# Nearest 2x upsampling on one core: half of the input as two equal loads from two queues

## The chip, the core and the metric

The kernel runs on one core of one Trainium2 chip. The metric is the device time of one launch in microseconds (us); lower is better. The core has 16 DMA engines, which all transfers share. DMAs are issued here from three engines' queues: SyncE's (SP), ScalarE's (ACT) and GpSimd's (POOL). The copies are made by VectorE (DVE) and ScalarE. TensorE does no work.

## The reference

The input x is float32 of shape (16, 64, 64, 64), the scale factor is 2. Every pixel is repeated in a 2 by 2 block:

```python
result = np.zeros((batch, channels, 2 * h, 2 * w), dtype=np.float32)
for i in range(2 * h):
    for j in range(2 * w):
        result[:, :, i, j] = x[:, :, i // 2, j // 2]
```

So 16.78 MB are read and 67.11 MB written, and nothing is calculated.

## The kernel before

All image rows of x (16 x 64 x 64 of them, 64 pixels or 256 bytes each) are spread over the 128 partitions: partition p has R = 512 rows, which lie next to each other in HBM, 128 KB in all. In the output the same partition has 512 KB next to each other. One tile `mem` in each partition holds a free stretch of WF elements and, behind it, all of the partition's input, `xt`.

**Loads** (line 195). Four loads, all issued by SyncE, bring x in by ranges of rows in each partition, cut at 0, 8, 256, 480 and 512. In each partition that makes pieces of 2 KB, 62 KB, 56 KB and 8 KB. They are called loads 0 to 3 below. They wait for nothing. After the program is built, `begin_before_barrier` (line 13) takes the first EARLY = 4 instructions of SyncE, which are these loads, and puts them ahead of the barrier at the program's start.

**Copies** (lines 215 and 216). The 512 rows are worked through in nine groups of 52, 40, 52, 63, 52, 64, 63, 63 and 63 rows. In each group VectorE expands the first 9/16 of the rows and ScalarE the rest; each makes from a row of 64 pixels two rows of 128, so that a group of k rows fills k x 1 KB in each partition. The first group covers rows 0 to 52, the second rows 52 to 92, the third rows 92 to 144.

**Where the copies go.** Groups with an even number (0, 2, 4, 6, 8) go to the start of `mem`. Groups with an odd number go to a place that ends at the group's own first input row, over input that earlier groups have used up. A group at the start of `mem` must wait until the store of the group before it in that place has read its data, and the same holds for the other place, so two stores can be on their way at a time.

**Stores** (lines 218 and 222). Each group's store follows its copies. Groups 0, 1, 7 and 8 are stored from SyncE's queue, groups 2 to 6 from GpSimd's. The store of group 0 has one more dependency, added by hand: it waits for `loads[-2]`, which is the load of rows 256 to 480, so that stores begin as the loads end. SyncE issues in order, so store 1 stands behind store 0.

`close_early` (line 80) rewrites the program's end; the change doesn't touch it.

Of the kernel before, what the change touches and what calls it, by code (L numbers as in the profile page):

```python
# [6 lines left out]

EARLY = 4  # L10


def begin_before_barrier(nc):

    blocks = nc.main_func.blocks
    main, body = blocks[0], blocks[1]
    sp = mybir.EngineType.SP
    loads = [i for i in body.instructions if i.engine == sp][:EARLY]  # L20
    for load in loads:
        assert isinstance(load, mybir.InstDMACopy), type(load)
        assert not (load.sync_info and load.sync_info.on_wait)
    names = [i.name for i in loads]
    body.instructions = [i for i in body.instructions if i.name not in names]
    kept = list(main.instructions)
    at = next(
        n
        for n, i in enumerate(kept)
        if i.engine == sp and isinstance(i, mybir.InstDrain)  # L30
    )
    kept[at:at] = loads
    main.instructions = kept


def close_on_gpsimd(nc):
# [117 lines left out]
@with_exitstack  # L154
def kernel(
    ctx: ExitStack,
    tc: tile.TileContext,
    x: bass.AP,
    scale_factor: int,
    out: bass.AP,  # L160
):
    nc = tc.nc
    nc.at_finalize(begin_before_barrier)
    nc.at_finalize(close_early)
    P = nc.NUM_PARTITIONS
    s = int(scale_factor)
    B, C, H, W = x.shape
    R = B * C * H // P
    fdt = x.dtype

    xp = x.rearrange("b c h w -> (b c h) w").rearrange("(p r) w -> p r w", p=P)
    op = out.rearrange("b c (h hd) w -> (b c h) (hd w)", hd=s).rearrange(
        "(p r) w -> p r w", p=P
    )

    rows = [52, 40, 52, 63, 52, 64, 63, 63, 63]
    GROW = s * s
    FREE = 79
    WF = FREE * GROW * W
    assert sum(rows) == R
    mem_pool = ctx.enter_context(tc.tile_pool(name="mem", bufs=1))
    mem = mem_pool.tile([P, WF + R * W], fdt, name="mem")
    xt = mem[:, WF:].rearrange("p (r w) -> p r w", r=R)

    HEAD = 8
    cuts = [0, HEAD, R // 2, R - 32, R]
    loads = [
        nc.sync.dma_start(out=xt[:, lo:hi], in_=xp[:, lo:hi])  # L195
        for lo, hi in zip(cuts, cuts[1:])
    ]

    def expanded(r0, r1):
        return (  # L200
            xt[:, r0:r1].unsqueeze(2).unsqueeze(4).to_broadcast([P, r1 - r0, s, W, s])
        )

    r0 = 0
    before = (0, 0)
    for n, k in enumerate(rows):
        size = k * GROW * W
        at = 0 if n % 2 == 0 else WF + r0 * W - size
        assert at >= before[1] or at + size <= before[0]
        before = (at, at + size)  # L210
        u = mem[:, at : at + size].rearrange(
            "p (k a w b) -> p k a w b", k=k, a=s, w=W
        )
        kv = k * 9 // 16
        nc.vector.tensor_copy(out=u[:, :kv], in_=expanded(r0, r0 + kv))  # L215
        nc.scalar.copy(out=u[:, kv:], in_=expanded(r0 + kv, r0 + k))  # L216
        if 2 <= n < len(rows) - 2:
            store = nc.gpsimd.dma_start(  # L218
                out=op[:, r0 : r0 + k, :], in_=u, single_packet=True
            )  # L220
        else:
            store = nc.sync.dma_start(out=op[:, r0 : r0 + k, :], in_=u)  # L222
        if n == 0:
            tc.add_manual_dep(
                store.ins,
                loads[-2].ins.name,
                mybir.DependencyInfo(
                    mybir.DependencyClass.Sync, mybir.DependencyReason.DATA
                ),
                reason="stores begin as the loads end",  # L230
            )
        r0 += k
# [35 lines left out]
```

## Time and profile before

| | before |
|---|---|
| median of 3 runs | 197.26 us (197.16 to 197.34) |
| span of the profiled execution, first to last instruction | 195.8 us |
| between the span and the median of the runs | 1.5 us |
| DMA: packets, bytes, mean rate over the span | 1872, 83.89 MB, 428 GB/s |
| VectorE busy | 69.6 us (36%), 9 copies |
| ScalarE busy | 51.4 us (26%), 9 copies and a table load |
| GpSimd busy | 3.0 us (2%) |

The profile is one execution. Of it only the span is listed; the execution's own time on the device is not shown beside it, so the 1.5 us between the span and the median of the runs stand for what lies around the span. The busy time of the DMA engines is given by queue as a share of all 16 engines' span: q1 is the queue that SyncE issues to, q0 GpSimd's. A packet is one partition's row of one transfer, and 4 bytes for each engine of a transfer that report its end.

### The profile page before, as it was taken

What the parts mean: (1) busy time and instruction counts of PE and PEld (TensorE: products, weight loads), DVE (VectorE), ACT (ScalarE), POOL (GpSimd) and SP (SyncE); (2) the same over time, 40 slices, a digit from 0 to 9 for tenths busy, and PEclk for the clock granted to TensorE, in tenths of its full rate; (3) what the DMA queues carried; (4) which work ended last, traced back from release to release, by engine and by line L of the source; (5) the groups of instructions that cost most, each with busy time, mean ns of one, the idle gap of its engine ahead of it and who ended that gap; (6) DMA issues with size and microseconds to landing.
All of it is one profiled execution on the core that took longest, in us unless ns stands there. A gap on an engine that the chain in (4) does not pass through costs nothing.

```text
span 195.8 us, 108 instructions
## 1 busy us (share of the span) xinstructions
DVE 69.6 (36%) x9; ACT 51.4 (26%) x10; POOL 3.0 (2%) x9
## 2 busy tenths in 40 slices
DVE  0000596000039289069007205930692002960000
ACT  2000548000036083063920006666000003900000
POOL 0000000000000100100100100010000000000000
DMA  9999889699899989899999899999999999999994
GB/s 391 493 415 415 375 387 551 295 455 522 348 442 418 537 370 500 370 422 422 422 422 522 348 522 428 428 428 428 422 422 422 422 422 422 448 514 501 435 422 211
DMA packets 1872, 83.89 MB, mean 428 GB/s; under 512 B 208, under 2 KB 208, under 8 KB 336
## 3 DMA queue, kind: packets, MB, share of 16 engines
q1 hardware_dynamic: 1152, 45.35, 53.8%
q0 software_dynamic: 720, 38.54, 45.4%
HBM read 16.78 MB, written 67.11 MB: 428 GB/s over the span
## 4 chain that ended last, share of the span: by engine, by line
DMA 73%; DVE 15%; issue 1%; SPq 1%; DVEq 0%; POOLq 0%
DMA out_dram<-mem 54%; DMA mem<-in_x_dram 19%; DVE mem L215 15%; SPq L195 0%; SPq L222 0%; DVEq L215 0%; POOLq L218 0%; POOLq L263 0%
## 5 line engine op out<-in xcount | busy, mean ns | idle before, releaser
L215 DVE COPY mem<-mem 128x8960 f32<-128x8960 f32 (+3 forms) x9 | 69.6, 7739 | 104.9 <-DMA out_dram<-mem 83.1
L216 ACT COPY mem<-mem 128x7168 f32<-128x7168 f32 (+2 forms) x9 | 50.1, 5572 | 117.5 <-DMA out_dram<-mem 89.8
L218 POOL DMA_DIRECT2D out_dram<-mem x5 | 2.8, 560 | 126.8 <-DVE mem L215 111.2
L216 ACT ACT_TABLE_LOAD x1 | 1.3, 1283 | 2.2 <-PEq L249 2.2
L249 POOL MEMSET const-float32-0.0<- 128x1 f32 x1 | 0.1, 99 | 0.2 <-issue 0.2
L249 POOL MEMSET const-bfloat16-1.0<- 128x1 bf16 x1 | 0.1, 102 | 0.0
L249 POOL MEMSET const-float32-1.0<- 128x1 f32 x1 | 0.1, 99 | 0.0
L249 POOL MEMSET const-uint8-127<- 128x1 uint8 x1 | 0.1, 99 | 0.0
## 6 DMA issues: line engine op xcount, KB each, us to landing
out_dram<-mem POOLq DMA_DIRECT2D x2, 8064.0 KB, 29.9
out_dram<-mem SPq DMA_DIRECT2D x2, 8064.0 KB, 24.8
out_dram<-mem POOLq DMA_DIRECT2D x2, 6656.0 KB, 22.6
mem<-in_x_dram SPq DMA_DIRECT2D x1, 7936.0 KB, 21.3
mem<-in_x_dram SPq DMA_DIRECT2D x1, 7168.0 KB, 37.8
out_dram<-mem SPq DMA_DIRECT2D x1, 6656.0 KB, 18.1
out_dram<-mem SPq DMA_DIRECT2D x1, 5120.0 KB, 29.7
mem<-in_x_dram SPq DMA_DIRECT2D x1, 1024.0 KB, 39.8
```

The source lines that it names most:

```text
L215: nc.vector.tensor_copy(out=u[:, :kv], in_=expanded(r0, r0 + kv))
L216: nc.scalar.copy(out=u[:, kv:], in_=expanded(r0 + kv, r0 + k))
L218: store = nc.gpsimd.dma_start(out=op[:, r0 : r0 + k, :], in_=u, single_packet=True)
L249: nc = _bacc.Bacc("TRN2", target_bir_lowering=False, num_devices=1)
```

## The change

The four loads are cut at 0, 128, 256, 480 and 512 rows, so that the first half of x comes as two loads with pieces of 32 KB in each partition. The second of these, rows 128 to 256, is issued by ScalarE; the others stay with SyncE. The function that moves loads ahead of the barrier now does so for two engines: three loads of SyncE and one of ScalarE. The last two loads, and with them the dependency of store 0, are as before. Copies and stores are untouched.

```diff
-EARLY = 4
+EARLY = {mybir.EngineType.SP: 3, mybir.EngineType.Activation: 1}
...
-    loads = [i for i in body.instructions if i.engine == sp][:EARLY]
...
+    for engine, count in EARLY.items():
+        loads = [
+            i
+            for i in body.instructions
+            if i.engine == engine and isinstance(i, mybir.InstDMACopy)
+        ][:count]
+        assert len(loads) == count
+        assert not any(i.sync_info and i.sync_info.on_wait for i in loads)
+        names = [i.name for i in loads]
+        body.instructions = [i for i in body.instructions if i.name not in names]
+        kept = list(main.instructions)
+        at = next(
+            n
+            for n, i in enumerate(kept)
+            if i.engine == engine and isinstance(i, mybir.InstDrain)
+        )
+        kept[at:at] = loads
+        main.instructions = kept
...
-    HEAD = 8
-    cuts = [0, HEAD, R // 2, R - 32, R]
+    cuts = [0, R // 4, R // 2, R - 32, R]
+    queues = [nc.sync, nc.scalar, nc.sync, nc.sync]
     loads = [
-        nc.sync.dma_start(out=xt[:, lo:hi], in_=xp[:, lo:hi])
-        for lo, hi in zip(cuts, cuts[1:])
+        queue.dma_start(out=xt[:, lo:hi], in_=xp[:, lo:hi])
+        for queue, lo, hi in zip(queues, cuts, cuts[1:])
     ]
```

More of the change, by code (lines that the diff above doesn't have):

```diff
@@ L18, in begin_before_barrier @@
     main, body = blocks[0], blocks[1]
-    sp = mybir.EngineType.SP
-    loads = [i for i in body.instructions if i.engine == sp][:EARLY]
[L21 to L33, printed above, removed]
+    for engine, count in EARLY.items():
[16 more added lines that the diff above has]
+        main.instructions = kept
 def close_on_gpsimd(nc):
```

## The prediction

> **What bounds the kernel now.** I read the page's busy slices and queue shares first, then the DMA issues, then the chain of waits in order of time, then the timeline of the first 40 us, and last the trace's records of single DMA packets (one record is one partition's row on one of the 16 DMA engines).
>
> ```profile
> DMA  9999889699899989899999899999999999999994
> DMA packets 1872, 83.89 MB, mean 428 GB/s; under 512 B 208, under 2 KB 208, under 8 KB 336
> q1 hardware_dynamic: 1152, 45.35, 53.8%
> q0 software_dynamic: 720, 38.54, 45.4%
> HBM read 16.78 MB, written 67.11 MB: 428 GB/s over the span
> ```
>
> 53.8% and 45.4% make 99.2%: the DMA engines are busy for all but 1.6 us of the 195.8 us span, while VectorE is busy 36% and ScalarE 26%. The digits under 9 among the slices come from whole rows being booked at one moment; in the packet records each engine starts its next row 2 to 20 ns after the last, from the first load to the last store. The kernel is bound by the bytes, and the loads are the first fifth of them.
>
> ```profile
> mem<-in_x_dram SPq DMA_DIRECT2D x1, 7936.0 KB, 21.3
> mem<-in_x_dram SPq DMA_DIRECT2D x1, 7168.0 KB, 37.8
> mem<-in_x_dram SPq DMA_DIRECT2D x1, 1024.0 KB, 39.8
> mem<-in_x_dram SPq DMA_DIRECT2D x1, 256.0 KB, 2.6
> ```
>
> The last column is the time from issue to landing. With SyncE's four issues at 0, 0.42, 0.89 and 1.36 us the loads land at 2.64, 21.74, 38.68 and 41.16 us. Load 2 (7168 KB, 7.34 MB) takes 16.94 us behind load 1: 433 GB/s. That is the full rate, and by it all 83.89 MB need 193.6 us.
>
> ```profile
> 0.89 37.79 DMA mem<-in_x_dram
> 38.68 0.02 issue
> ...
> 39.29 29.69 DMA out_dram<-mem
> ...
> 79.15 40.20 DMA out_dram<-mem x2
> ...
> 129.52 35.38 DMA out_dram<-mem
> ```
>
> The chain runs from load 2 into store 0 and from there through later stores and three copies. Each copy in it (9.5 us on VectorE) has another transfer beside it, which is why the DMA engines never pause although the chain names VectorE for 15%.
>
> ```profile
> 0.00 1.80 SPq L195 DMA_DIRECT2D mem<-in_x_dram  x4
> ...
> 2.20 1.28 ACT L216 ACT_TABLE_LOAD   x1 [2.20 <-PEq L249]
> 21.77 5.10 ACT L216 COPY mem<-mem 128x5888 f32<-128x5888 f32 x1 [18.29 <-DMA mem<-in_x_dram]
> 21.84 10.89 DVE L215 COPY mem<-mem 128x7424 f32<-128x7424 f32 x2 [21.84 <-DMA mem<-in_x_dram]
> 29.81 4.03 ACT L216 COPY mem<-mem 128x4608 f32<-128x4608 f32 x1 [2.95 <-DVE mem L215]
> 38.77 136.12 SPq L222 DMA_DIRECT2D out_dram<-mem  x4
> ```
>
> Both engines start their first copies as load 1 lands and are through the first two row groups at 33.84 us (29.81 + 4.03). Store 0 then waits 4.9 us more for load 2, by the dependency set in the code.
>
> **How much there is to win.** The first packet starts at 1.0 us, and the last store's data ends 0.4 us before the span does. Between them lie 195.8 - 1.0 - 0.4 = 194.4 us against 193.6 us at the full rate, so 0.8 us are lost on the whole. They are lost at the very start. Load 0 (0.262 MB) needs 0.61 us at the full rate; its packets begin at 1.005 us and the slowest engine's end at 2.289 us, 0.68 us too long: six engines show a first row of 2 KB that took 368 to 587 ns where the later ones took 84. Load 1 needs 18.75 us and lands 19.10 us after load 0: 0.35 us too long, and its records show where: the first row of 62 KB takes 2382 to 3082 ns, 2680 on the mean, against 2342 for nearly all that follow. The slowest engine loses 1.0 us by this, the mean engine 0.8 us. From load 2 on nothing is lost: its rows take 2116 ns from the first, 27.1 bytes per ns.
>
> **The change part by part.**
>
> Bytes and number of loads stay: 32 + 32 + 56 + 8 KB of each partition's row in place of 2 + 62 + 56 + 8, four loads both times. At the full rate the sum for the loads is the same 38.7 us. Zero, and nothing has to hide it.
>
> Issue. SyncE loses one of four issues (0.43 us) and ScalarE gains one. SyncE's last load is issued at about 0.89 us instead of 1.36 us; it is served only after 37.8 us, so these 0.47 us are worth nothing. ScalarE's issue lies ahead of the barrier that releases it at 2.12 us in the trace of before; it reaches that barrier 0.13 us into the span, so an issue of about 0.4 us fits. Its table load follows the barrier and ends by 3.5 us, and its first copy comes 18 us later. If that cover were gone, it would cost the issue's 0.4 us. Its load is ready at about 1.2 to 1.6 us, while SyncE's first row of 32 KB keeps each engine until at least 1.0 + 1.2 = 2.2 us (32,768 bytes at 27.1 per ns). So no engine waits for ScalarE's issue.
>
> [...]
>
> Landing order. In the stretch from 152.5 to 162 us of before, where a store of GpSimd's queue and one of SyncE's run together, each engine serves one row of the one queue and one of the other, in turn, at 2380 to 2404 ns a row against 2380 alone. By that row loads 0 and 1 share the engines evenly and land together, after 64 KB per partition: 8.39 MB at 433 GB/s is 19.4 us, plus 1.0 us for the first packet, up to 1.0 us of the start and 0.35 us of completion, 21.0 to 21.8 us. The first two row groups (rows 0 to 92) now need load 0 alone; they are ready at about 33.1 to 33.9 us, still 5 us ahead of load 2. Row group 2 (rows 92 to 144) needs both and waits for store 0's space until 56.9 us anyway. Load 2 has the same bytes ahead of it, whatever the order, and store 0 the same load ahead of it; load 3's 1.05 MB (2.4 us) still covers store 0's issue, which came 38.77 us in while the engines were busy with load 3 to 40.3 us.
>
> The start. This is the one term that can move. The trace of before has no cold first row of 32 KB and no two loads side by side. From below: if a cold start with large rows pays only what load 1's first row paid, 0.35 us, the 0.68 us of the small load go away: -0.68 us. From above: if the whole 1.0 us is the price of sixteen engines starting on HBM at once, whatever the row, and ScalarE's queue pays a first row of its own at the mean excess of load 1's (2680 - 2342 = 0.34 us), the change costs +0.34 us. I take the row that is nearest, the cold start as one whole, paid once: 1.0 us before and 1.0 us after, less 8 rows at 84 against 76 ns, -0.07 us. I round that to nothing, since the unevenness between engines alone is 0.5 us there.
>
> Row switches between the queues: 16 rows per engine, each between 0 and 24 ns more by the mixed stores, 0 to 0.4 us. Most of those rows were at 2380, so I take 0.05 us.
>
> Sum: 0 + 0 - 0.07 + 0.05, about no change on a span of 195.8 us. The runs shown have a median of 197.26 us, 1.5 us above the span, which I leave as it is: 197.3 us. About 0.2% (0.4 us) is what a measurement of this kernel can tell from no change.
>
> **The rivals.**
>
> Faster: the 2 KB rows are the cost. For it: six of sixteen first small rows are 4 to 7 times too long, and a big row has time to hide such a delay. Against: the big rows behind them were again up to 0.74 us late, as if the start were shared and not the small rows' own. Price -0.68 us, 196.6 us.
>
> Slower: ScalarE's queue starts cold in the middle of SyncE's stream, and reads from HBM switch queues less freely than the stores did. Place: the first 20 us. Price: the first row of the second queue costs 0.34 us (mean) to 0.74 us (3082 - 2342, worst engine), and 16 switches up to 24 ns add up to 0.4 us: 0.4 to 1.1 us, 197.7 to 198.4 us. It decides from a loss of 0.025 us per row on each engine (16 rows, 0.4 us). [...] A fixed price for a second hardware queue outside the span would end on the same side. Against: mixed stores show almost nothing.
>
> Slower by far: SyncE's queue is served ahead of ScalarE's. Then load 1 would come only after loads 0, 2, 3 and stores 0 and 1 (24.6 MB, 57 us), and row group 2 would be copied with idle engines: 9.7 us of load 1, then 7.9 us of copy uncovered, about +8 us, 205 us. Against: the even turns of the two stores.
>
> The change not doing what it says: ScalarE's load after the barrier, at 2.2 us rather than 0.1. Eight rows of load 0 keep every engine until at least 10 us, so nothing changes; this is within the forecast.
>
> **How the numbers follow.** No change to be told 0.42; the small rows' price gone, faster, 0.22; the second queue's price, slower, 0.34; starvation, slower, 0.02. The range takes the faster end at 196.6 us and the slower rival up to 198.2 us; what is beyond each end I hold at 1 in 10.
>
> **What would show it.** Right: DMA slices at 9 throughout, loads 0 and 1 landing within about 1.5 us of each other near 21 us, load 2 at 38.4 to 39.0 us, store 0 issued right after, first copies near 21.5 us, and the end shifted by as much as load 2's landing. Wrong on the start: load 2's landing moved by more than 0.4 us, with first rows of 32 KB far from 1.2 us. Wrong on the switches: rows in the first 20 us longer than 1.21 us all along. Wrong outside: an equal span and another time. Wrong on the order: load 0 landing at 11 us, with load 1 either at 21 us (harmless) or after the first stores.

## Result: 0.28% slower, by what the stores lost

The changed kernel has a median of 197.95 us over 22 executions (197.77 to 198.31), the kernel before 197.23 us over 22 on the same chip. The ratio is 1.0028, with a 95% interval of 1.0019 to 1.0038: slower, by more than the 0.2% that count as no change. The executions of before come in two groups, which the numbers below need: 15 of the 22 lie between 197.03 and 197.34 us (short, below) and the others from 197.59 us upwards (long), while the changed kernel has none under 197.77 us. The profile of before fits the first group: its span is 195.8 us, and the changed kernel's profiled execution took 197.91 us on the device with a span of 196.58 us, 1.33 us around it, which puts the profiled execution of before at 197.1 us.

These lines of the page of the changed kernel answer to those of before:

```profile
DMA  8999999799899989899999899999999999999994
DMA packets 1873, 83.89 MB, mean 427 GB/s; under 512 B 209, under 2 KB 209, under 8 KB 209
q1 hardware_dynamic: 1008, 41.16, 48.8%
q0 software_dynamic: 720, 38.54, 45.5%
q10 hardware_dynamic: 144, 4.19, 4.9%
```

A third queue, q10, carries ScalarE's 4.19 MB. The three shares still sum to 99.2%: the DMA engines are as busy as before, for a span that is 0.8 us longer. So they are not idle for that time; they take longer for the same bytes.

Its DMA issues (KB each, us from issue to landing) and the start of its timeline:

```profile
mem<-in_x_dram SPq DMA_DIRECT2D x1, 7168.0 KB, 38.4
mem<-in_x_dram SPq DMA_DIRECT2D x1, 4096.0 KB, 21.9
mem<-in_x_dram ACTq DMA_DIRECT2D x1, 4096.0 KB, 21.9
mem<-in_x_dram SPq DMA_DIRECT2D x1, 1024.0 KB, 40.4
```

```profile
0.00 1.32 SPq L196 DMA_DIRECT2D mem<-in_x_dram  x3
0.12 0.38 ACTq L196 DMA_DIRECT2D mem<-in_x_dram  x1
...
21.89 10.89 DVE L216 COPY mem<-mem 128x7424 f32<-128x7424 f32 x2 [21.89 <-DMA mem<-in_x_dram]
29.87 4.03 ACT L217 COPY mem<-mem 128x4608 f32<-128x4608 f32 x1 [2.88 <-DVE mem L216]
38.89 136.73 SPq L223 DMA_DIRECT2D out_dram<-mem  x4
```

The change does what it says: ScalarE issues 0.12 us in, and both halves land together, at 21.87 and 22.04 us. VectorE's first copy begins 0.05 us later than before, and the copies of the first two row groups are through 5 us ahead of store 0's issue. Load 2 lands at 38.80 us (before: 38.68), load 3 at 41.28 us (before: 41.16).

The chain of waits, in order of time, shows where the rest comes from:

```profile
0.43 38.37 DMA mem<-in_x_dram
...
39.36 29.87 DMA out_dram<-mem
...
79.41 40.53 DMA out_dram<-mem x2
...
130.10 35.55 DMA out_dram<-mem
```

Leg by leg against before: load 2 lands 0.12 us later; store 0 takes 29.87 us for 29.69 (+0.18), the next two stores 40.53 for 40.20 (+0.33), the next 35.55 for 35.38 (+0.17). Together 0.80 us, the whole difference of the spans. The copies between the legs are the same. Five sixths of the loss fall into stores, which the change didn't touch.

The packet records say how (a record is one partition's row; the records don't name the engine, so I joined each to the one that ended just before it; where two engines end within a few ns of each other this can take one for the other, so counts and sums over all engines are surer than what is said of a single one). Store 0's rows of 52 KB: 1966 ns for every one of 128 in the kernel before, 1974 ns on the mean in the changed one. Store 1's rows of 40 KB: 1514 against 1522 ns. It begins with store 0's first row on each engine: in before, each engine goes from load 3 into store 0 within 6 ns; in the changed kernel 13 of the 16 first rows are 34 to 48 ns too long, and the engines had run out of load 3 for 0.11 us on the mean before their store rows came. Of store 0's later rows 78% are 2 to 12 ns too long (before: none), and it goes on so to the end. Each engine has 72 store rows. Beyond the row times of 1966, 1514, 2380 and 2418 ns (the usual times of rows of 52, 40, 63 and 64 KB), these add up to 0.61 us on the mean engine after the change and to 0.09 us before. Of the 0.61 us, 0.25 us lie in rows that are 1 to 12 ns too long, 0.15 us in rows 13 to 30 ns too long, and 0.21 us in 58 rows, the 13 first ones among them, that are 31 to 105 ns too long.

On the mean engine, then: 0.01 us from the loads, 0.11 us of idling ahead of store 0 and 0.52 us in store rows; and the slowest engine, which sets the end, lies 0.34 us behind the mean one, where it was 0.16 us.

### The profile page after: what moved, and what is told of

Same layout as the page of the kernel before. It is cut to its first block, busy times and chain, and to the rows that moved or that the text cites. A ratio compares the mean times of both kernels' runs of the same rounds, so it can differ in the third digit from the quotient of the medians.

```text
span 196.6 us, 108 instructions
## 1 busy us (share of the span) xinstructions
DVE 69.6 (35%) x9; ACT 51.4 (26%) x10; POOL 3.0 (2%) x9
## 3 DMA queue, kind: packets, MB, share of 16 engines
q1 hardware_dynamic: 1008, 41.16, 48.8%
q10 hardware_dynamic: 144, 4.19, 4.9%
## 4 chain that ended last, share of the span: by engine, by line
DMA 73%; DVE 14%; issue 1%; SPq 0%; DVEq 0%; POOLq 0%
DMA out_dram<-mem 54%; DMA mem<-in_x_dram 20%; DVE mem L216 14%; SPq L223 0%; SPq L196 0%; DVEq L216 0%; POOLq L219 0%; POOLq L264 0%
```

## Experiments

Three theories were on the table. A: ScalarE's queue, once used, costs at every later row. B: without the small first load the engines stand to each other so that their store rows collide. C, formed on the first four runs: store 0's rows reach some engines after these have run out of load 3, and such an engine pays at every row afterwards. The comparisons of each set ran on one chip, with the kernel before beside them.

**First set: which part of the change?**

Of the kernel before beside this set 14 of 29 executions lie at 196.99 to 197.22 us and 15 at 197.51 to 199.48. By the medians, then, three of the four runs can't be told from it: the ratios are 1.0001 for the halves from SyncE, 1.0008 for the small load from ScalarE and 1.0000 for the half from GpSimd, each with an interval of 0.0022 to either side. What they say rests on their profiles, and on how many of their executions are long.

Halves from SyncE alone:

```diff
-EARLY = {mybir.EngineType.SP: 3, mybir.EngineType.Activation: 1}
+EARLY = {mybir.EngineType.SP: 4}
-    queues = [nc.sync, nc.scalar, nc.sync, nc.sync]
+    queues = [nc.sync, nc.sync, nc.sync, nc.sync]
```

> The loads are cut into 32 + 32 + 56 + 8 KB rows as in the changed kernel, but all four are issued by SyncE; ScalarE's queue is not used. Theory A (once ScalarE's queue has been used, every later row on a DMA engine costs 5 to 8 ns more, 72 store rows each engine): store rows are back at 1966 ns (52 KB) and 1514 ns (40 KB), time within 0.1 us of before, 197.2 us. Theory B (the small first load sets the engines apart in a way in which their store rows don't collide, whatever the queue): store rows stay at about 1974 and 1522 ns on the mean and the time at 197.8 to 198.0 us.

Measured: 197.73 us median; 3 of 12 executions at 197.05 to 197.17 us, the others at 197.67 to 197.85. In the profile (an execution of 197.73 us) store 0's rows take 1969 ns and 5 engines have a long first row. Neither A nor B as stated: without ScalarE's queue store rows are too long on some engines and 9 of 12 executions are long, and the other quarter takes the time of before's short ones with the 32 KB rows in place.

The cuts of before, with load 1 on ScalarE's queue:

```diff
-    cuts = [0, R // 4, R // 2, R - 32, R]
+    cuts = [0, 8, R // 2, R - 32, R]
```

> The loads are cut into 2 + 62 + 56 + 8 KB rows as before; load 1 (62 KB rows) alone moves to ScalarE's queue. Theory A (ScalarE's queue): store rows at about 1974 and 1522 ns, time 197.8 to 198.0 us. Theory B (the small first load): rows of 1966 and 1514 ns, 197.2 us. Here SyncE's loads 2 and 3 also run beside load 1, so load 2 lands earlier relative to the end of the loads; by both theories this moves the time by less than 0.2 us, since the DMA engines stay busy.

Measured: 205.08 us. My remark that loads 1 and 2 side by side would move the time by less than 0.2 us was wrong, as its page and timeline show:

```profile
GB/s 386 425 380 467 492 380 380 386 0 335 502 335 425 515 425 335 502 525 418 405 405 370 502 335 540 412 412 412 409 405 507 507 405 405 405 405 405 456 557 203
```

```profile
38.95 5.10 ACT L217 COPY mem<-mem 128x5888 f32<-128x5888 f32 x1 [35.93 <-DMA mem<-in_x_dram]
38.95 10.89 DVE L216 COPY mem<-mem 128x7424 f32<-128x7424 f32 x2 [38.95 <-DMA mem<-in_x_dram]
46.91 135.74 SPq L223 DMA_DIRECT2D out_dram<-mem  x4
```

Load 1 shares the engines with load 2 and lands at 38.9 us together with it. The first copy begins only then, store 0 is issued at 46.91 us in place of 38.77, and the DMA engines stand still in the ninth slice. In this kernel the first copies need everything up to row 52, and load 1 has that. The run tells nothing about A and B; it shows that a load moved to the second queue no longer lands ahead of the load that stood behind it.

The small load alone on ScalarE's queue:

```diff
-    cuts = [0, R // 4, R // 2, R - 32, R]
-    queues = [nc.sync, nc.scalar, nc.sync, nc.sync]
+    cuts = [0, 8, R // 2, R - 32, R]
+    queues = [nc.scalar, nc.sync, nc.sync, nc.sync]
```

> As before in cuts; the small load of 2 KB rows alone moves to ScalarE's queue, which then has 0.26 MB to bring and nothing after 3 us. Theory A in its plain form (the queue's having been used is enough): store rows at about 1974 and 1522 ns, 197.7 to 198.0 us. Theory B (the engines' places after the start decide): the small rows are still there, but beside the 62 KB rows and not ahead of them, so a time between 197.2 and 197.9 us, with the store rows slow or not according to how the engines stand to each other.

Measured: 197.87 us, all 12 executions at 197.77 to 198.00. Load 2 lands at 38.81 us, 10 engines have a long first row in store 0, and its rows take 1973 ns. That is what A in its plain form expected, and B allowed it; this run doesn't decide between them.

Rows 128 to 256 from GpSimd's queue:

```diff
-EARLY = {mybir.EngineType.SP: 3, mybir.EngineType.Activation: 1}
+EARLY = {mybir.EngineType.SP: 3}
-    queues = [nc.sync, nc.scalar, nc.sync, nc.sync]
+    queues = [nc.sync, nc.gpsimd, nc.sync, nc.sync]
```

> As the changed kernel, but rows 128 to 256 are loaded from GpSimd's queue, behind the barrier, and not from ScalarE's. The stores use GpSimd's queue anyway, so no third queue is ever used. Theory A (ScalarE's queue): store rows at 1966 and 1514 ns, 197.2 us. Theory B (no small first load): slow store rows, 197.8 to 198.0 us. If any second queue in the load phase spoils the stores: slow rows too, and then it is the first run that tells which.

Measured: 197.73 us, one execution of 12 at 197.05, the others at 197.57 to 197.86. Three engines have a long first row in store 0; store 0's rows take 1968 ns on the mean, more than A expected and less than B. Joined by engine, 3 engines have 0.56 to 0.72 us too much in their 72 store rows and the other 13 at most 0.14 us. In the run with the halves from SyncE it is 5 engines with 0.52 to 0.82 us and 11 with at most 0.32 us. So it takes few engines: the slowest sets the end, and the times of both kernels agree though one has 3 slow engines and the other 5. This led to theory C.

**Second set: is it store 0's arrival?**

The changed kernel with store 0 issued as soon as its copies are made, and the same edit to the kernel before:

```diff
-        if n == 0:
+        if False:
             tc.add_manual_dep(
```

> The changed kernel without the hand-made dependency of store 0 on load 2: store 0 is issued as soon as its copies are made, at about 30 us, and stands behind loads 2 and 3 in SyncE's queue. Theory C (in the changed kernel store 0's rows reach 11 of 16 engines after these have run out of load 3; such an engine idles 0.1 to 0.7 us and from then on pays about 5 ns at every row): no engine pauses ahead of store 0, its rows take 1966 ns and store 1's 1514 ns from the first, and the time falls to 197.0 to 197.3 us. Theory B (the engines' places after a start without the small load make the rows collide): store 0's rows stay at about 1974 ns and the time at 197.8 to 198.0 us. Theory A (ScalarE's queue once used): as B.

> The kernel before without the hand-made dependency of store 0. Theory C: in its profile no engine paused ahead of store 0, but only just; of its other executions a part is 0.6 to 1.0 us longer, which would be those in which some engines did. With store 0 queued 8 us earlier all executions lie at 197.0 to 197.3 us. Theories A and B: no difference to the kernel before, with the same mixture of times.

The timeline of the first shows the edit:

```profile
29.94 143.79 SPq L223 DMA_DIRECT2D out_dram<-mem  x4
```

and its DMA issues what it led to:

```profile
mem<-in_x_dram SPq DMA_DIRECT2D x1, 7168.0 KB, 38.5
mem<-in_x_dram SPq DMA_DIRECT2D x1, 1024.0 KB, 41.5
```

Measured: 198.31 us for the changed kernel so edited (ratio to before 1.0049, 1.0030 to 1.0067) and 198.87 us for the kernel before (1.0078, 1.0049 to 1.0107). C was right about the rows and wrong about the time. Every row of store 0 takes 1966 ns and every one of store 1 1514 ns, no engine pauses, and all 72 store rows of an engine together have 0.01 us too much, where the changed kernel had 0.61 us; ScalarE's queue and the 32 KB rows are still there. So neither is enough to make the rows slow, and A and B fall as they stood. But load 3 lands at 42.41 us, 3.5 us behind load 2 (38.89 us) in place of 2.5. Load 3's rows of 8 KB take 309 ns in the changed kernel without exception; here they begin at 309 ns, rise to 580 ns on the mean in the sixth row, and lose 0.91 us per engine. With store 0's rows queued behind them, the last rows of the loads run at half speed. In the kernel before, so edited, they lose 1.07 us, and its profiled execution (199.49 us) shows another thing: the first row of store 2, GpSimd's first, takes 3092 to 3512 ns on 15 engines, in place of 1966.

The kernel before with a shorter load 3, and the changed kernel with a longer one:

```diff
-    cuts = [0, HEAD, R // 2, R - 32, R]
+    cuts = [0, HEAD, R // 2, R - 16, R]
```

> The kernel before with load 3 at 4 KB rows and load 2 at 60 KB, so that half as many bytes (1.2 us in place of 2.4 us) lie between load 2's landing and the end of the loads. Theory C: all 16 engines run dry by about 1 us ahead of store 0, all first rows are about 40 ns longer and the later ones about 5 to 10 ns: 1.0 + 0.6 us, 198.4 to 199.2 us. Theories A and B: the small first load and SyncE's queue are as before, so only the pause counts, 1966 ns rows, 198.0 to 198.4 us.

```diff
-    cuts = [0, R // 4, R // 2, R - 32, R]
+    cuts = [0, R // 4, R // 2, R - 64, R]
```

> The changed kernel with load 3 at 16 KB rows and load 2 at 48 KB: 4.8 us of bytes behind load 2 and the dependency kept. Theory C: store 0's rows are there 2 us before any engine runs out, so rows of 1966 and 1514 ns and 197.0 to 197.3 us. Theories A and B: slow rows, 197.8 to 198.0 us.

Measured: 209.42 us and 198.38 us. The short load 3 also turned the order of two stores round in the built program: store 1 stands ahead of store 0 in SyncE's queue and is issued at 33.83 us.

```profile
33.83 153.17 SPq L222 DMA_DIRECT2D out_dram<-mem  x4
54.67 9.49 DVE L215 COPY mem<-mem 128x8960 f32<-128x8960 f32 x1 [21.98 <-DMA out_dram<-mem]
70.26 5.10 ACT L216 COPY mem<-mem 128x5888 f32<-128x5888 f32 x1 [36.46 <-DMA out_dram<-mem]
```

Row group 2 waits for store 0's space, which is now free only at 70 us in place of 57, while the engines have run dry. That is where the 12 us went; the run tells nothing about the pause. The long load 3 agrees with the early store: store rows perfect (0.01 us too much), load 3's rows of 16 KB 611 ns at first and 1195 ns on the mean in the seventh row, 1.10 us lost per engine. So there is a price on both sides: store rows that come 2 us early cost 0.9 to 1.1 us of the loads, and those that come late cost the pause and the later rows.

The profiles side by side, from the packet records of one execution each:

| kernel | its time, us | long first rows of store 0 | rows of store 0, ns | excess of an engine's store rows, us | loss in load 3's rows, us |
|---|---|---|---|---|---|
| before | about 197.1 | 0 of 16 | 1966.0 | 0.09 | 0 |
| changed | 197.91 | 13 | 1974.4 | 0.61 | 0 |
| small load from ScalarE | 197.78 | 10 | 1972.5 | 0.49 | 0 |
| halves from SyncE | 197.73 | 5 | 1969.2 | 0.28 | 0 |
| half from GpSimd | 197.60 | 3 | 1967.9 | 0.16 | 0 |
| changed, store 0 early | 198.35 | 0 | 1966.0 | 0.01 | 0.91 |
| changed, load 3 of 64 rows | 198.48 | 0 | 1966.0 | 0.01 | 1.10 |

The excess is a mean over the 16 engines; the time goes by the slowest one, which is why it falls less from 13 late engines to 3 than the mean does.

One count needs no joining by engine: the share of store 0's rows, after the first row of each engine, that are too long at all. It goes with the number of long first rows: 79% with 13 of 16, 60% with 10, 29% with 5, 17% with 3, and none with none. So an engine with a long first row goes on with long rows.

**Third set: is there a place between?**

The changed kernel with 0.30 us more behind load 2:

```diff
-    cuts = [0, R // 4, R // 2, R - 32, R]
+    cuts = [0, R // 4, R // 2, R - 36, R]
```

> The changed kernel with load 3 at 36 image rows (9 KB) in place of 32 and load 2 at 220: load 2 lands 0.30 us earlier against the end of the loads (each image row is 8 x 256 bytes per engine, 0.076 us). Theory C2 (store 0's rows must reach each engine just as it runs out of load 3: later, the engine idles and pays about 5 ns a row from then on; much earlier, the last rows of load 3 take up to twice as long): of the 11 to 13 engines that paused in the changed kernel at most 4 still do, store 0's rows are below 1969 ns on the mean, and the time is 197.2 to 197.6 us, unless load 3's last rows already grow over 309 x 9/8 = 348 ns. Theory A (ScalarE's queue once used costs at every row): 197.8 to 198.0 us.

Measured: 197.62 us (197.14 to 197.96); 4 of 12 executions at 197.14 to 197.24, the others from 197.59. The ratio to before is 1.0008 (0.9991 to 1.0026). In the profile (an execution of 197.80 us) load 3's rows are still at 347 ns, one engine in place of 13 has a long first row, and store 0's rows take 1966.7 ns. One engine has 0.81 us too much in its store rows, the other 15 have 0 to 0.26 us, and that one ends 0.60 us after the next. Of store 0's later rows 5% are too long, about one engine's share. The median is just above the 197.2 to 197.6 us that C2 expected.

The edit of four image rows took 13 late engines down to 1 and brought a third of the executions to the times of before, with ScalarE's queue and equal halves in place. It doesn't beat the kernel before.

The small load in front of the equal halves:

```diff
-EARLY = {mybir.EngineType.SP: 3, mybir.EngineType.Activation: 1}
+EARLY = {mybir.EngineType.SP: 4, mybir.EngineType.Activation: 1}
-    cuts = [0, R // 4, R // 2, R - 32, R]
-    queues = [nc.sync, nc.scalar, nc.sync, nc.sync]
+    cuts = [0, 8, R // 4, R // 2, R - 32, R]
+    queues = [nc.sync, nc.sync, nc.scalar, nc.sync, nc.sync]
```

> The changed kernel with the 2 KB rows of before as a load of their own in front, from SyncE: 2 + 30 KB rows from SyncE, 32 KB from ScalarE, 56 and 8 KB from SyncE. Theory B2 (the small first load brings the engines into the order in which a load's or a store's rows are handed out, so that store 0's reach each engine in its turn): no or few engines pause, 197.1 to 197.4 us. Theory C2 without B2 (only the distance between load 2's landing and the end counts): as the changed kernel, 8 or more engines pause, 197.7 to 198.0 us.

Measured: 198.05 us (197.87 to 198.23), ratio 1.0040 (1.0025 to 1.0054). Load 2 lands at 38.98 us, 9 engines have a first row that is 15 to 42 ns too long, and the store rows have 0.66 us too much on the mean engine. The small first load by itself doesn't bring the kernel back; B2 falls.

This profile also shows a limit of C2. The engines idle for only about 0.02 us on the mean ahead of store 0, against 0.11 us in the changed kernel, and the excess is as large. Of store 0's rows 54% are too long, of store 1's 67%, of store 2's 91% and of store 3's 98%: engines that began store 0 without a long row became slow later.

The kernel before with 0.15 us less, and with 0.15 us more, behind load 2:

```diff
-    cuts = [0, HEAD, R // 2, R - 32, R]
+    cuts = [0, HEAD, R // 2, R - 30, R]
```

> The kernel before with load 3 at 30 image rows and load 2 at 226: 0.15 us less between load 2's landing and the end of the loads, about what the changed kernel lost (its load 2 landed 0.12 us later, its first engine ran out 0.03 us earlier). Theory C2: 8 or more engines pause ahead of store 0, later rows cost 4 to 8 ns more, and all executions lie at 197.7 to 198.1 us, without the change's loads and without ScalarE's queue. Theories A and B: as before, 197.0 to 197.4 us for most.

```diff
-    cuts = [0, HEAD, R // 2, R - 32, R]
+    cuts = [0, HEAD, R // 2, R - 34, R]
```

> The kernel before with load 3 at 34 image rows and load 2 at 222: 0.15 us more between load 2's landing and the end. Theory C2: no engine pauses in any execution, so the times of 197.6 us and more that the kernel before shows in a third of its executions are gone, and all lie at 197.0 to 197.3 us; if store rows that come 0.15 us early already slow load 3's last rows, up to 0.2 us more. Theories A and B: the same mixture as before.

Measured, 0.15 us less: 197.85 us, ratio 1.0024 (1.0013 to 1.0036); 10 of 12 executions at 197.54 to 198.02, where of the kernel before beside it 6 of 29 are that long. Two image rows, with neither ScalarE nor equal halves, cost 0.68 us at the median, about as much as the change. The profile fell on one of the two short executions (197.26 us), and in it no engine pauses and store 0's rows take 1966 ns, as C2 has it for a short one. That the long executions paused is thus not shown by any trace.

Nor does load 2's landing alone decide: it came at 38.96 us in this profile, 0.28 us later than in that of before, without a pause, while the run ahead has 9 long first rows with a landing at 38.98 us. And rows become too long without a pause here as well, none in stores 0 and 1 but 59% in store 5, together 0.23 us on the mean engine.

Measured, 0.15 us more: 197.24 us, ratio 1.0010 (0.9997 to 1.0023); 7 of 12 at 197.07 to 197.29, but 5 at 197.75 to 198.16. That the long executions would vanish was wrong. The profile fell on one of them (198.16 us): no pause, store 0's rows 1966 ns, but 8 engines take 3194 to 3513 ns for the first row of store 2, 1.2 to 1.5 us too much. The long executions of a kernel can thus have another cause than the pause.

## Why the prediction was right or wrong

The forecast was no change, 197.3 us, with 196.6 to 198.2 as the range. The time lies in the range, but 0.65 us above the forecast, and it is slower by 0.28%, the case that had 0.34. That it lies in the range is luck: the upper end was set by the slower rival, whose mechanism didn't happen.

**The start** was right. The term I left at nothing came out at 0.01 us on the mean engine (load 3 ended at 40.535 us on the mean before, at 40.545 after). The cold first row of 32 KB took 1814 ns on the mean, 0.6 us too long, once; the loads end at the same time in both kernels all the same, so the faster rival, by which large rows would hide the cold start, is refuted.

**The row switches** I put at 0.05 us cost nothing: SyncE's and ScalarE's rows alternate one by one, at 1213 ns each, 27.0 bytes per ns. ScalarE's first row took 1211 ns, no cold start of its own. So the slower rival had the size (0.4 to 1.1 us) and the sign, but its place, the first 20 us, and its mechanism are refuted. On each of the 16 engines one partition's row of the one queue follows one of the other, eight of each, and the landings at 21.87 and 22.04 us follow from it.

Two readings of the records in the prediction were slightly off, and nothing hangs on them: in the stretch from 152.5 to 162 us no row takes more than 2395 ns (2404 there), and most store rows begin 4 ns before the record of the last one ends, not 2 to 20 ns after it.

**Issue and landing order** were right, 0.1 to 0.2 us late: both halves at 21.87 and 22.04 us against 21.0 to 21.8 forecast, first groups ready at 33.9 us.

**The step that failed** is the sentence that load 3's 1.05 MB (2.4 us) still covers store 0's issue. I compared the issue (38.77 us) with the end of load 3 (40.3 us on the first engine) and took the 1.5 us between as cover to spare. The records say otherwise: in the changed kernel store 0's first rows started 1.48 to 2.04 us after the issue instruction began, 13 of 16 of them long. In the kernel before they started 1.50 to 2.02 us after it, on each engine within 6 ns of its last load row. With the delays of the changed kernel, then, the cover was used up already, and load 2 landing 0.12 us later, and the first engine running out 0.03 us earlier, was enough. The delay is not the same in every execution, though: in the profile with 30 rows in load 3 they began 1.36 to 1.86 us after the issue, and no engine waited for them. So that there was little to spare is shown; that these 0.12 us tipped the balance is an estimate from the two profiles. By the prediction's own sign the end was to shift by as much as load 2's landing, 0.12 us; it shifted by 0.80 us. I also had the evenness between engines as something to round away ("0.5 us there"), while load 2's landing waits for the slowest engine (its 16 reports came at 38.22 to 38.80 us in the changed kernel, and store 0 was issued at 38.89 us) and load 3's cover ends with the fastest (40.24 us); the spread of the engines at the end of load 3 went from 0.52 to 0.62 us.

**What the cover was worth** was missing from the sum as well. In the changed kernel a pause of 0.11 us on the mean goes with 0.5 us of longer rows later. The early store and the long load 3, which take the pause away and leave the loads' queues alone, took the 0.61 us of row excess to 0.01 us. That is shown, and so is that an engine with a long first row goes on with long rows. Why it does, and over 150 us, is not; nor is the pause the only way there, since rows also turned slow later, on engines that hadn't paused, with 30 rows in load 3 and with the small load in front.

**Left open.** All 22 executions of the changed kernel and all 12 with the small load on ScalarE's queue are long, while the two kernels with equal halves and no ScalarE queue have 4 short ones in 24. Whether that is the 0.1 us by which load 2 lands later with ScalarE's queue (38.80 and 38.81 us against 38.70 and 38.65) or something more of that queue, the runs don't settle; the 4 short executions with 36 rows in load 3 and ScalarE's queue in use speak for the first, but the two landings at 38.96 and 38.98 us, one without and one with long first rows, say that the landing is not all. Nor is the number of long first rows an exact measure: 13 of them go with 0.61 us of row excess, 9 with 0.66 us. What makes a part of the executions of before long is open too; the profiles of its variants show one cause, the slow first row of store 2.

The 1.5 us that I put around the span were 1.33 us for the profiled execution, since it belonged to the shorter group.

## What to carry to other kernels

When transfers of two kinds follow each other on saturated DMA engines, look at the place where the one kind hands over to the other, engine by engine, before looking at the start: here the issue had to be early enough for the engine that ran out first (at 40.24 us in the changed kernel, where the first store row of any engine began 1.48 us after the issue at 38.89 us), while its trigger was the landing on the engine that was last (38.80 us). A margin that holds in one profile can be nothing to spare; two groups of times in the runs of one kernel can be a sign of it, though here one long execution had another cause. And a chain by legs, laid beside that of the other kernel, shows quickly whether a small loss sits in what was changed or in what comes after it.

## What the runs showed of the hardware

- In the changed kernel the DMA engines idled for 0.11 us on the mean between loads and stores. 13 of 16 took 34 to 48 ns too long for their first store row, and 78% of the rows of store 0 that followed were 2 to 12 ns too long. With 36 rows in load 3 one engine of 16 did so and ended 0.6 us after the next.
- Rows also turned slow later on engines that hadn't paused (0.23 us on the mean engine in a profile without a pause). With store 0 of the changed kernel queued 2 us or more ahead of the loads' end, rows kept their usual times up to the last store, but for 0.01 us.
- Stores queued on the same queue behind loads slowed the loads' last rows to about half speed (309 ns to 580 ns for 8 KB, 611 to 1195 ns for 16 KB), 0.9 to 1.1 us per engine, before that engine's first store row began.
- In the changed kernel, store 0's first rows began 1.48 to 2.04 us after SyncE's issue instruction, with 0.55 us between the first engine and the last.
- In two profiled executions the first row of GpSimd's first store took 3.1 to 3.5 us in place of 1.97 on 8 and 15 of the engines. The cause is open.
